# Encoder block in float32: half-size sums in DRAM for every second pair of w_down's rows, made during gate and up; fewer of h's sums through one buffer

## The chip, the cores and the metric

One core of one Trainium2 chip. The metric is the device time in microseconds of one execution; the kernel before has a median of 1118.89 us over three runs (1118.12 to 1121.63).

## What is computed

One block of a bidirectional encoder with 256 tokens and 16 meta tokens, width 2048, all in float32. Attention (neighbourhood attention in 8 heads, latent attention in 8 heads, an output projection) is followed by a gated MLP with 5632 inner columns, which is what the change touches:

```python
def conv_glu(x, w_gate, w_up, conv_w, conv_b, w_down):
    g = x @ w_gate
    u = x @ w_up
    ...
    for i in range(CONV_W):
        gc = gc + conv_w[i] * gp[:, i:i + L]
    return (jax.nn.silu(gc) * u) @ w_down

h = h + mix @ w_out[l]
h = h + conv_glu(rmsnorm(h, ffn_norm_g[l]), w_gate[l], w_up[l], conv_w[l], conv_b[l], w_down[l])
```

## The kernel before

**Splits.** TensorE multiplies in a float32 form of lower precision, so each operand is split into a high and a low part and each product becomes two or three matmuls. Every weight goes through one pipeline: SP issues a load of 512 KB into a buffer `raw` (128x1024), ACT copies it to `whi` (rounded), DVE subtracts to get `wlo`, TensorE uses both. There are five `raw` buffers, four `whi` and four `wlo`. When the MLP begins one more raw buffer is added (`more_raw`), and when gate and up no longer need the normed input, eight more (`halves`). A raw buffer is free again after DVE's subtraction.

**Strassen-like products.** Some parts of up (`w_up_s`, five groups of four column tiles, QUADS) and of down (`w_down_m`, 512 columns, called "mid"; `w_down_s`, 1024 columns, called "down") take seven products of sums in place of eight. The sums are of two kinds. Sums of values: `value_sums` takes four differences on DVE and splits them on ACT and DVE into a 128x1024 tile; for h (pairs 0 to 7 of its 16 tiles, `hl_sums`) and for the MLP's inner values (22 pairs, `pair_sums`). Most of these tiles are built in the one buffer `sums` (pool `combined`), stored to DRAM (`s_up`, `s_down`), and loaded again into `sin` (pool `s_parts`) when the products need them; `sums` is free when its store has landed. h's sums are also kept near, in the last columns of `act`, the tile of inner values, until those are written. That tile takes over the memory of attention's buffers, so it is there only from `ev_mlp` on. Before, pairs 0 to 5 (`EARLY = ST // 2`) go through `sums` and are loaded back into `act` after `ev_mlp`; pairs 6 and 7 wait for `ev_mlp` and are built in `act` itself.

Sums of weights (`weight_sums`): a row pair of `w_down_s` has four quarters of 512 columns. Two sums of neighbouring quarters are made in DRAM ahead of time (`sums_in_dram`): SP copies two quarters (512 KB) of the weights to a DRAM tile `early`, and a DMA issued on POOL adds the next two quarters to it (an accumulate). In the last stage the pair loads its lower quarters (512 KB, `lower`), one upper quarter (256 KB, `upper`) and the early tile (512 KB, `two`), and DVE makes two further sums of 128x512 in a fourth buffer (`more`).

**Stages.** Attention runs to about 395 us, with the output projection at its end; gate and up follow, with the groups of seven products spread among them; from about 765 us the 22 pairs of mid are spread among the last gate and up tiles; from about 955 us the 22 pairs of down stand among 13 of the 24 pieces of `w_down`'s other 512 columns (done the plain way), seven pieces having gone ahead, and the last four stand at the end. The copies and accumulates of `sums_in_dram` start in attention (first copy at 39 us, last accumulate at 378 us).

**What sets the order.** The kernel is written as threads that a small planner (`Flow`) runs with modelled costs: each instruction is recorded when the planner's clock of its engine says so, and all engines then run that order. So SP is one queue in a fixed order, and so are ACT and DVE: an instruction that waits holds all behind it. Threads with a low priority (3), such as h's sums, are recorded when nothing else is ready in the model, but in the chip they hold the engine like any other. A helper's line stands for all its uses: L243 is every ACT activation, L247 every DVE two-operand instruction, L283 and L661 to L663, L1955, L1956 the matmuls, L514 every load and store issued by SP, L716 the accumulate on POOL.

The waits on the small `scr` tiles in attention are copies between partitions that are issued on SP among the weight loads (rotary keys and queries); `sq8r` are squares of a head, which TensorE adds up.

## Time and profile before

| | |
|---|---|
| median of three runs | 1118.89 us (1118.12 to 1121.63) |
| the profiled execution | 1123.05 us, of which the span is 1121.2 |
| TensorE busy in the span | 98% |
| DVE, ACT, POOL busy | 90%, 67%, 13% |
| mean granted TensorE clock | 0.997 |
| DMA traffic | 275.57 MB, mean 246 GB/s |

A busy TensorE in this profile is not TensorE at its peak, since ends of matmuls are modelled; its waits are read from what ended them. "Idle before" stands in brackets behind an instruction, with what released it. A stage is read by the busy time of each engine in its window: where TensorE's has no gap, only work taken from TensorE or a faster clock can shorten the stage.

### The profile page before, as it was taken

What the parts mean: (1) busy time and instruction counts of PE and PEld (TensorE: products, weight loads), DVE (VectorE), ACT (ScalarE), POOL (GpSimd) and SP (SyncE); (2) the same over time, 40 slices, a digit from 0 to 9 for tenths busy, and PEclk for the clock granted to TensorE, in tenths of its full rate; (3) what the DMA queues carried; (4) which work ended last, traced back from release to release, by engine and by line L of the source; (5) the groups of instructions that cost most, each with busy time, mean ns of one, the idle gap of its engine ahead of it and who ended that gap; (6) DMA issues with size and microseconds to landing.
All of it is one profiled execution on the core that took longest, in us unless ns stands there. A gap on an engine that the chain in (4) does not pass through costs nothing.

```text
span 1121.2 us, 22349 instructions
## 1 busy us (share of the span) xinstructions
PE 1102.6 (98%) x8164; PEld 1048.7 (94%) x8164; DVE 1008.2 (90%) x1907; ACT 755.9 (67%) x1518; POOL 142.8 (13%) x216
## 2 busy tenths in 40 slices
PE   9989999999999989999999999999999999999998
PEld 9989999999999989999999999999999999787777
DVE  8869887988878879999999999999998989999896
ACT  8678978888647666656656556655665565666664
POOL 3221212232334400000000000000000000301012
PEclk9999999999999999999999999999999999999999
DMA  8666878687887888665756667567797889799991
GB/s 323 226 202 196 217 196 239 190 223 225 280 256 214 234 276 301 204 212 174 257 172 202 229 210 267 200 215 271 268 316 268 283 280 372 280 321 322 336 308 66
DMA packets 83318, 275.57 MB, mean 246 GB/s; under 512 B 9352, under 2 KB 13448, under 8 KB 83208
## 3 DMA queue, kind: packets, MB, share of 16 engines
q1 hardware_dynamic: 79752, 262.34, 68.3%
q0 software_dynamic: 3168, 11.54, 6.4%
q8 instruction: 64, 1.05, 0.4%
q14 instruction: 46, 0.38, 0.1%
q10 hardware_dynamic: 288, 0.27, 0.1%
HBM read 255.61 MB, written 40.89 MB: 264 GB/s over the span
## 4 chain that ended last, share of the span: by engine, by line
PE 73%; DVE 11%; DMA 9%; ACT 3%; issue 2%; SPq 1%; POOL 0%; DVEq 0%; ACTq 0%; POOLq 0%
PE bank L283 17%; PE bank L661 14%; PE bank L662 14%; PE bank L663 14%; PE bank L1955 8%; DVE wlo L247 7%; PE bank L1956 4%; PE bank L289 2%; DMA raw<-in_w_down_m 1%; DMA halves<-early 1%; DMA raw<-early 1%; ACT whi L243 1%; DMA scr<-scr 1%; DMA more_raw<-early 1%; DVE raw L247 1%
## 5 line engine op out<-in xcount | busy, mean ns | idle before, releaser
L243 ACT ACTIVATE whi<-raw 128x512 fp32r<-128x512 f32 (+2 forms) x511 | 381.1, 765 | 138.8 <-PE bank L662 49.2
L247 DVE TENSOR_TENSOR wlo<-raw,whi 128x512 fp32r<-128x512 f32 (+2 forms) x511 | 444.7, 891 | 26.5 <-ACT whi L243 25.4
L661 PE MATMUL bank<-hl,whi 128*128 128x258 f32 (+1 forms) x1208 | 347.8, 288 | 0.0
L662 PE MATMUL bank<-hl,whi 128*128 128x258 f32 (+1 forms) x1208 | 344.4, 285 | 0.0
L663 PE MATMUL bank<-hl,wlo 128*128 128x258 f32 (+1 forms) x1208 | 344.0, 285 | 0.2
L663 PEld LDWEIGHTS bank<-hl,wlo 128*128 128x128 f32 x1208 | 230.4, 191 | 0.9 <-DVE wlo L247 0.8
L662 PEld LDWEIGHTS bank<-hl,whi 128*128 128x128 f32 x1208 | 229.9, 190 | 0.1
L661 PEld LDWEIGHTS bank<-hl,whi 128*128 128x128 f32 x1208 | 229.0, 190 | 0.4
L283 PE MATMUL bank<-whi,act 128*128 128x256 f32 (+1 forms) x560 | 144.4, 308 | 0.0
L1955 PE MATMUL bank<-hl,whi 128*128 128x512 f32 x384 | 138.1, 398 | 0.0
L1956 PE MATMUL bank<-hl,wlo 128*128 128x256 f32 x384 | 108.4, 282 | 0.6 <-DVE wlo L247 0.6
L283 PEld LDWEIGHTS bank<-whi,act 128*128 128x128 f32 x560 | 98.9, 189 | 5.9
L271 POOL TENSOR_TENSOR mt<-mt,mt 128x256 f32<-128x256 f32 x3 | 3.5, 1168 | 675.6 <-ACT mt L243 675.6
L243 ACT ACTIVATE whi<-halves 128x1024 fp32r<-128x1024 f32 (+2 forms) x68 | 63.5, 944 | 37.7 <-PE bank L283 22.4
L1955 PEld LDWEIGHTS bank<-hl,whi 128*128 128x128 f32 x384 | 72.9, 190 | 15.1
L283 PE MATMUL bank<-wlo,act 128*128 128x256 f32 (+1 forms) x280 | 86.2, 308 | 0.0
L283 PE MATMUL bank<-whi,sin 128*128 128x256 f32 (+1 forms) x312 | 85.0, 326 | 0.1
L247 DVE TENSOR_TENSOR wlo<-halves,whi 128x1024 fp32r<-128x1024 f32 (+2 forms) x68 | 75.0, 1124 | 1.0 <-ACT whi L243 0.6
L1956 PEld LDWEIGHTS bank<-hl,wlo 128*128 128x128 f32 x384 | 73.2, 191 | 0.9 <-DVE wlo L247 0.9
L243 ACT ACTIVATE whi<-more_raw 128x1024 fp32r<-128x1024 f32 (+2 forms) x60 | 51.6, 868 | 23.1 <-PE bank L283 6.4
L247 DVE TENSOR_TENSOR wlo<-more_raw,whi 128x1024 fp32r<-128x1024 f32 (+2 forms) x60 | 58.5, 987 | 3.2 <-ACT whi L243 3.2
L283 PEld LDWEIGHTS bank<-whi,sin 128*128 128x128 f32 x312 | 55.3, 188 | 6.1 <-issue 0.3
(301 smaller groups left out, 2166.9 us busy)
## 6 DMA issues: line engine op xcount, KB each, us to landing
raw<-in_w_gate SPq DMA_DIRECT2D x72, 512.0 KB, 5.5
raw<-in_w_in SPq DMA_DIRECT2D x52, 512.0 KB, 4.8
raw<-in_w_up SPq DMA_DIRECT2D x39, 512.0 KB, 6.0
sin<-s_down SPq DMA_DIRECT2D x36, 512.0 KB, 6.3
raw<-in_w_out SPq DMA_DIRECT2D x32, 512.0 KB, 5.9
raw<-in_w_up_s SPq DMA_DIRECT2D x32, 512.0 KB, 4.5
early<-in_w_down_s SPq DMA_DIRECT2D x22, 512.0 KB, 6.4
early<-in_w_down_s POOLq DMA_DIRECT2D x22, 512.0 KB, 7.9
```

The costliest lines, as they stand in the source:

```text
L243: nc.scalar.activation(out, in_, f, **kw)
L247: nc.vector.tensor_tensor(out, a, b, op)
L271: nc.gpsimd.tensor_tensor(out, a, b, op)
L283: nc.tensor.matmul(o, l, r, start=start, stop=stop)
L289: nc.tensor.transpose(o, i, ident[:n, :n])
L661: nc.tensor.matmul(ps, whi, xhi, start=start, stop=False)
L662: nc.tensor.matmul(ps, whi, xlo, start=False, stop=False)
L663: nc.tensor.matmul(ps, wlo, xhi, start=False, stop=stop)
L1955: nc.tensor.matmul(ps, whi, x, start=start, stop=False)
L1956: nc.tensor.matmul(ps[:, :n], wlo, x[:, 0, :], start=False, stop=stop)
```

## The change

- The DRAM sums start at `ev_mlp`, not in attention, with 18 us between steps, not 12.
- Pairs of `w_down_s` with an odd number ("third") have one early sum of 512 columns (256 KB copied, 256 KB added). It is loaded into the first half of `upper`, the raw upper quarter into the second, as two loads of 256 KB; the load of `two` goes, and DVE makes three sums of 128x512, not two. Even pairs are as before ("both").
- `EARLY = 4`: h's pairs 4 and 5 no longer go through `sums` and DRAM into `act`; they take a raw buffer as before, wait for `ev_mlp` in a thread of their own and are built in `act`, as pairs 6 and 7 are. They are stored afterwards.
- The sums of the last two pairs of values are used from where they were built in the mid stage: pair 20 from `sums`, pair 21 from a `sin` buffer (before: pair 21 alone, from `sums`).
- The last six mid pieces and the seven plain pieces ahead of down are ordered "mmdmmdddmmddd" (m mid, d plain), not "mmdmdmdmdmddd".
- The planner takes 2600 ns, not 2000, for a load's landing after 400 us of its clock, and counts the accumulates' traffic. Quarters have other product orders in "third" pairs; `MID_SUMS = 0` leaves the same for mid unused.

```diff
-MID_LEAD, MID_LEFT, MID_GAP = 4, 6, 2
+THIRD = 2
+MID_SUMS = 0
+EARLY_PACE = 18000.0
+LANDING = 2600.0
+MID_LEAD, TAIL = 4, "mmdmmdddmmddd"
...
+            if r.mode == "both":
+                yield "sp", 600
+                load(r.at["upper"][:, :q], r.src[:, :q], r.first_loaded, nc.sync)
+            else:
+                src, done = early_sums[r.g]
+                yield done
+                yield "sp", 600
+                load(r.at["upper"][:, :q], src, Event(), nc.sync)
+                yield "sp", 600
+                load(r.at["upper"][:, q:], r.src[:, :q], r.first_loaded, nc.sync)
...
                 yield r.first_loaded
+                yield from TT(m[:, :q], up[:, :q], up[:, q:], ALU.add)
+                r.used("upper")
+                yield from TT(m[:, q:], m[:, :q], low[:, q:], ALU.add)
+                yield from TT(t[:, :q], m[:, :q], low[:, :q], ALU.subtract)
...
+    for g in range(FC // 2):
+        ev, q, w = Event(), PW // 2, io["w_down_s"][g]
+        if g % THIRD:
+            t = dpool.tile([P, q], F32, name=f"early{g}")
+            early.append((t, w[:, q : 2 * q], w[:, 2 * q : 3 * q], ev))
+        else:
+            t = dpool.tile([P, PW], F32, name=f"early{g}")
+            early.append((t, w[:, : 2 * q], w[:, q : 3 * q], ev))
...
-            fl.cur.t += 12000.0
+            fl.cur.t += EARLY_PACE
...
-        yield pieces[18].loaded
-        fl.spawn(sums_in_dram())
...
         fl.set(ev_mlp)
+        fl.spawn(sums_in_dram())
...
-    EARLY = ST // 2
+    EARLY = 4
...
+            if EARLY <= i < ST // 2:
+                fl.spawn(hl_pair(i, v, ab), 3)
+            else:
+                yield from hl_pair(i, v, ab)
+    def hl_pair(i, v, ab):
+        if i >= EARLY:
+            yield ev_mlp
+        yield from value_sums(*saved_sums["up"][i], *ab, near[i])
...
-            parts = yield from one(combined)
+            parts = yield from one(s_parts if last == [LAST] else combined)
```

What the planner makes of it, at three places. First SP in attention, where the third early copy stood ahead of four scr copies. Before:

```order
L514 DMA raw1_81<-in_w_kv_up 128x512
L514 DMA raw2_82<-in_w_in 128x1024
L514 DMA raw3_83<-in_w_in 128x1024
L514 DMA early2_137<-in_w_down_s 128x1024
L514 DMA scr8_184<-scr6_182 32x258 x4
L514 DMA raw4_84<-in_w_in 128x1024
```

The same place of the change:

```order
L540 DMA raw1_81<-in_w_kv_up 128x512
L540 DMA raw2_82<-in_w_in 128x1024
L540 DMA raw3_83<-in_w_in 128x1024
L540 DMA scr1_177<-scr7_183 32x258 x4
L540 DMA raw4_84<-in_w_in 128x1024
```

The copy is gone and the scr copies stand behind weight loads alone; as in all of attention, buffer numbers differ.

Second ACT where the MLP begins; `s_2` is the norm's scale, `resT` the residual, `raw` with `res` the gained h of a pair. Before:

```order
L243 ACTIVATE parts_sq0_194<-kr_202 128x258
L243 ACTIVATE raw4_84<-res4_4086,vecs_94 128x256
L243 ACTIVATE whi3_88<-raw2_82 128x1024
L243 ACTIVATE resT4_5374<-bank7_79 128x512
L243 ACTIVATE sums0_93<-raw4_84 128x256
L243 ACTIVATE s_2_165<-scr8_184 128x258
L243 ACTIVATE s_2_165<-s_2_165 128x258
L243 ACTIVATE scr3_179<-s_2_165 128x258
L243 ACTIVATE sums0_93<-raw4_84 128x256
L243 ACTIVATE whi0_85<-raw3_83 128x1024
```

The same place of the change:

```order
L247 ACTIVATE parts_sq0_194<-kr_202 128x258
L247 ACTIVATE raw4_84<-res4_4043,vecs_94 128x256
L247 ACTIVATE whi3_88<-raw2_82 128x1024
L247 ACTIVATE resT4_5329<-bank7_79 128x512
L247 ACTIVATE s_2_165<-scr3_179 128x258
L247 ACTIVATE s_2_165<-s_2_165 128x258
L247 ACTIVATE scr4_180<-s_2_165 128x258
L247 ACTIVATE raw2_82<-res5_4056,vecs_94 128x256 x2
L247 ACTIVATE whi0_85<-raw3_83 128x1024
```

Pair 4's two splits into `sums` no longer stand around the scale; those of pairs 1 to 3 stand ahead of these rows in both. Pair 5's gain moves one weight split earlier and holds its buffer, with pair 4's, until `act` is there.

Third DVE in the last stage, an even and an odd pair of the change:

```order
L251 TENSOR_TENSOR raw4_84<-raw4_84,halves3_11164 128x512
L251 TENSOR_TENSOR raw2_82<-halves2_11125 128x512
L251 TENSOR_TENSOR raw2_82<-raw2_82,halves2_11125 128x512
L251 TENSOR_TENSOR halves1_11086<-raw2_82,halves2_11125 128x512
L251 TENSOR_TENSOR wlo0_89<-halves3_11164,whi0_85 128x1024
L251 TENSOR_TENSOR wlo1_90<-halves1_11086,whi1_86 128x512
```

The first row is the second sum of an even pair; the next three are an odd pair's, where before there were two.

192 lines of the change are left out of this document (121 added, 71 removed).

## The prediction

> **What bounds the kernel now.** I read the page's first two sections, then the busy time by stage, then what TensorE waits for. Columns of the stage rows: window in us, length, then busy time and instruction count of PE, PEld (its weight loads), DVE, ACT and POOL, granted TensorE clock, DMA share, GB/s.
>
> ```profile
> span 1121.2 us, 22349 instructions
> PE 1102.6 (98%) x8164; PEld 1048.7 (94%) x8164; DVE 1008.2 (90%) x1907; ACT 755.9 (67%) x1518; POOL 142.8 (13%) x216
> ```
> ```profile
> 40.00:100.00 60.00, 56.94 (x450) 56.00 (x449) 46.81 (x125) 45.99 (x133) 10.02 (x20) 0.97 0.65 199
> 395.00:420.00 25.00, 22.04 (x139) 19.86 (x139) 18.63 (x36) 18.21 (x34) 0.30 (x1) 0.93 0.83 269
> 420.00:520.00 100.00, 100.00 (x779) 97.23 (x778) 93.90 (x175) 63.64 (x101) 0.00 (x0) 1.00 0.67 228
> 520.00:620.00 100.00, 100.00 (x809) 98.58 (x809) 98.33 (x180) 63.65 (x100) 0.00 (x0) 1.00 0.63 208
> 620.00:720.00 100.00, 99.61 (x770) 96.17 (x770) 96.14 (x182) 61.02 (x102) 0.00 (x0) 1.00 0.65 226
> 720.00:780.00 60.00, 59.91 (x469) 58.10 (x468) 58.31 (x106) 37.08 (x59) 0.00 (x0) 1.00 0.70 242
> 780.00:833.00 53.00, 53.00 (x387) 50.38 (x387) 51.12 (x95) 32.81 (x53) 0.00 (x0) 1.00 0.83 283
> ```
> ```profile
> 955.00:1095.00 140.00, 136.46 (x630) 109.53 (x629) 129.25 (x143) 91.09 (x105) 16.89 (x13) 1.00 0.90 318
> ```
> ```profile
> PE bank L283 <- DVE sq8r L259: 3.8, 3, 2.8
> PE bank L283 <- DVE wlo L247: 3.3, 5, 1.3
> ```
>
> TensorE bounds it nearly everywhere: in gate and up (420 to 780) it never rests, and DVE, at 94 to 98 of 100 us, keeps up only just. So no edit can win more than TensorE's waits and its slow clock. The waits sit in three places: one in attention (sq8r, 2.8), one where the MLP begins (3 us, rows in part 2), five small ones in the last stage (wlo, 3.3 together). The two rows above give TensorE's waits for one instruction each: sum, times, longest. The granted clock is below 1 in two rows: 0.03 x 60 = 1.8 us and 0.07 x 25 = 1.75 us, right behind the two long waits. The profiled execution took 1123.05 us, the span and 1.85 around it, 4.2 over the median of 1118.89.
>
> **1. Attention: DRAM sums leave it.** The long wait:
>
> ```profile
> 76.43 0.17 PE L283 MATMUL bank<-ones_r,sq8r 128*4 128x2 f32 x1 [2.82 <-DVE sq8r L259]
> 76.83 0.22 PE L283 MATMUL bank<-ones_r,sq8r 128*4 128x2 f32 x3 [0.24 <-POOL sq8r L271]
> ```
> ```profile
> 67.65 6.96 DMA scr<-scr
> ```
> ```profile
> 64.78 0.52 SPq L514 DMA_DIRECT2D early<-in_w_down_s  x1
> 65.82 2.42 SPq L514 DMA_DIRECT2D scr<-scr  x4
> ```
>
> TensorE rests 2.82 + 0.24 = 3.06 us because four small scr copies land late. A 512 KB early copy stood just ahead of them on SP, and an accumulate was issued on POOL beside them. The first row below gives the landing of these four, the second that of the next group, which had no early copy directly ahead.
>
> ```profile
> DMA to landing us min/median/max: 5.5/6.9/7.4
> ```
> ```profile
> DMA to landing us min/median/max: 3.7/4.8/5.2
> ```
>
> Medians differ by 2.1 us, and the early copy's issue (0.52) is gone as well: about 2.6 us sooner, bounds 0.5 (most of the wait is the weight loads ahead) and 3.06 (all). I take 2.3. Elsewhere in attention the order shifts by a few rows; TensorE's other waits there are about 1 us of sq8r. I take 0.5 gained, bounds -3 (one new wait like the old) and +2.
>
> **2. Where the MLP begins.** ACT rows first, with the wait in brackets, then DVE, then TensorE, then the chain.
>
> ```profile
> 369.31 0.42 ACT L243 ACTIVATE sums<-raw 128x256 fp32r<-128x256 f32 x1 [4.03 <-DMA s_up<-sums]
> 394.64 0.72 ACT L243 ACTIVATE sums<-raw 128x256 fp32r<-128x256 f32 x2 [1.81 <-DMA s_up<-sums]
> 403.22 0.42 ACT L243 ACTIVATE sums<-raw 128x256 fp32r<-128x256 f32 x1 [2.02 <-DMA s_up<-sums]
> ```
> ```profile
> 369.76 0.42 DVE L247 TENSOR_TENSOR sums<-raw,sums 128x256 fp32r<-128x256 f32 x1 [2.16 <-ACT sums L243]
> ```
> ```profile
> 399.42 0.39 PE L283 MATMUL bank<-parts_sq,ones_r 128*128 128x258 f32 x1 [2.06 <-ACT parts_sq L243]
> 400.71 0.39 PE L283 MATMUL bank<-parts_sq,ones_r 128*128 128x258 f32 x1 [0.90 <-DVE parts_sq L247]
> ```
> ```profile
> 387.36 7.19 DMA s_up<-sums
> ```
> ```profile
> DMA to landing us min/median/max: 6.8/7.3/9.1
> ```
>
> The last row gives the landing of the four saves from 360 to 396. Every pair of h's sums waits until the one `sums` buffer is saved, 7 us, and the weight splits behind it on ACT and DVE wait too. The edit frees pairs 4 and 5, so the 2.02 at 403 goes; but the waits that reach TensorE at 397 are those of pairs 1 to 3 (4.03 to 1.81), which keep the buffer. What helps these is the traffic that leaves: an accumulate, issued at 361.61, ran beside the first save, the one of 9.1 us, and POOL's issues slow DVE, which runs without a pause from 369.76 on:
>
> ```profile
> 355.94 0.75 DVE L247 TENSOR_TENSOR res<-res,scr 128x258 f32<-128x258 f32 x2
> 361.04 1.25 DVE L247 TENSOR_TENSOR res<-res,scr 128x258 f32<-128x258 f32 x2
> 372.05 0.88 DVE L255 SCALAR_TENSOR_TENSOR hl<-res,vecs,hl 128x258 fp32r<-128x258 f32 x2
> 376.93 1.38 DVE L255 SCALAR_TENSOR_TENSOR hl<-res,vecs,hl 128x258 fp32r<-128x258 f32 x2
> 302.53 3.86 DVE L247 TENSOR_TENSOR wlo<-raw,whi 128x512 fp32r<-128x512 f32 x3
> ```
> ```profile
> 361.61 0.79 POOL L716 DMA_DIRECT2D early<-in_w_down_s  x1
> 377.57 0.80 POOL L716 DMA_DIRECT2D early<-in_w_down_s  x1
> ```
>
> At each issue the same DVE pair takes 0.50 us more (1.25 against 0.75, 1.38 against 0.88). DVE comes 0.5 us earlier by the second issue and up to 2.16 by a faster first save; of TensorE's 2.06 + 0.90 = 2.96 us I take 2.2 as gained, bounds 0 and 2.96. Against it: pairs 4 to 7 now hold up to four weight buffers together while four 512 KB reloads and the first early copy queue, where before it was six reloads. Up to four split pieces of 24 products at 100/809 = 0.124 us, 11.9 us of TensorE's work, cover this; without them a late load would cost 2 us.
>
> **3. The slow clock.** It followed each rest of about 3 us and cost 3.55 us here; the rest of 1.3 us, in a row with clock 1.00, had none behind it. If 1 and 2 hold, both go. The profiled execution is 4.2 over the median, so I suppose that the median execution has it once: 1.8 gained, bounds 0 and 3.55. [...]
>
> **4. Gate and up take the DRAM sums.** In DMA time:
>
> ```profile
> q1 hardware_dynamic: 79752, 262.34, 68.3%
> q0 software_dynamic: 3168, 11.54, 6.4%
> ```
>
> An accumulate takes 6.4% x 1121.2 / 22 = 3.26 us of all 16 engines; a copy at q1's rate (262.34 MB in 766 us) 1.53, at most 3.26. With half the bytes in every second pair that is 22 x 0.75 x 4.8 = 79 us over 24 steps of 18 us: +0.18 on shares of 0.63 to 0.70. It fits, except from 780 to 833, where 0.83 + 0.18 is over 1. On DVE 22 issues cost 22 x 0.50 = 11 us. One a step is 5.6 per 100 us, 2.8 us, against idle time of 6.1, 1.7, 3.9 and (per 100) 2.8 and 3.5 in the rows above: DVE falls 1.1 us behind between 520 and 620 and recovers in the next row, inside the 11.9 us that it can work ahead. SP pays 0.52 a copy, which waits for nothing; the weight loads behind it start that much later, which the same pieces cover. POOL has no other work there. I take 1.0 lost in all, bounds 0 and 6 (79 us of DMA at the one tenth that doesn't fit from 780 on gives 5 of it). [...]
>
> **5. The last stage.** In every second pair a read of 256 KB goes (11 x 0.26 MB = 2.9 MB, 8.4 us at q1's rate) and one sum of 128x512 comes:
>
> ```profile
> L247 DVE TENSOR_TENSOR halves<-halves,raw 128x512 f32<-128x512 f32 x9 | 6.2, 686 | 2.1 <-DMA raw<-early 2.0
> ```
> ```profile
> DVE halves L247 <- DMA halves<-early: 4.5, 4, 1.5
> DVE halves L247 <- DMA raw<-early: 3.3, 2, 2.0
> DVE halves L247 <- DMA more_raw<-early: 1.1, 1, 1.1
> ```
>
> DVE gains 11 x 0.69 = 7.5 us of work and has 140 - 129.25 = 10.75 idle, 8.9 of it the waits above for early sums. Where these waits go, the work fits and TensorE's 3.3 us of waits go too; where they stay, it ends 7.5 - 1.85 = 5.6 later. DMA at 0.90 falls to 0.84, so I take 1.0 gained, bounds -5.6 and +3.3. The last values' sums in place and the order of the 13 pieces ahead of the stage cost nothing: TensorE shows no wait between 860 and 955, and ready pieces hide them; uncovered, one load of 7 us.
>
> **Sum.** 2.3 + 0.5 + 2.2 + 1.8 - 1.0 + 1.0 = 6.8 under the median: 1112. Against the profiled execution, with the whole 3.55, it is 8.55: 1114.5.
>
> **The rivals.**
> - *The waits stay.* The copies and saves are late because of weight loads ahead of them, not of early traffic, and pairs 1 to 3 keep the one buffer, so that the edit frees none that matters. For it: 7.19 at 387, when no accumulate ran. Then 1, 2 and 3 give nothing: 1118.9 - 0.5 = 1118.4.
> - *DVE becomes the bound in gate and up (slower).* Next to an issue at 303 three splits took 3.86 us, where three of 128x512 take 3 x 0.69 = 2.1 (the mean in part 5): 1.8 us lost, with POOL additions beside it. At 1.5 us an issue, 8.3 per 100 us, DVE would fall behind by 2.2 + 6.7 + 4.5 + 3.3 + 2.5 = 19 us in the five rows; half of the 11.9 of lead covers 6, 13 reach TensorE: 1118.9 - 7.8 + 13 = 1124. It reaches TensorE from about 1 us an issue (lateness 8.2, over the 6) and makes the kernel slower from about 1.25. Against it: POOL has no additions there.
> - *Everything goes*: 3.06 + 2.96 + 3.55 + 2 + 3.3 = 14.9: 1104.
>
> **Chances and range.** Forecast (1107 to 1115.5) 0.53, better 0.14, waits stay 0.20, slower 0.13. About 0.3%, 3.4 us, is what a measurement can tell from no change: faster 0.67, same 0.20, slower 0.13. The range runs from the best case, 1103.5, to 1122.5, short of the slower rival.
>
> **What would show it.** Right: scr copies landing in about 5 us and no clock below 1 at 77 and 402; ACT's waits for s_up under 2 us; DVE pairs longer by 0.5 at POOL's issues, with TensorE's count per 100 us unchanged; no DVE wait on early sums. Wrong: a gap of TensorE in gate and up, a new rest of 3 us in attention, or DVE without idle time behind 955.

## The result and the profile after

| | before | change |
|---|---|---|
| median of 20 runs each | 1121.62 us (1118.12 to 1124.88) | 1120.34 us (1118.23 to 1121.86) |
| profiled execution | 1123.05 us, span 1121.2 | 1118.23 us, span 1116.4 |
| ratio to before | | 0.9984, 95% interval 0.9974 to 0.9994 |

The change is faster by 0.16% (0.06 to 0.26% by the interval), less than the 0.3% that the prediction counted as no change. Six to seven us were forecast. The profiles are 4.8 us of span apart, the medians 1.3: the profiled execution of before lies 1.4 over its median, that of the change 2.1 under. Stages are read from one profiled execution of each kernel, so differences of a us or two between them are not safe; ratios decide.

**By stage.** The span is cut at three starts that each trace has: the first up product, the first down product 512 wide, the last such product.

| us | to the first up product | gate, up, change to down | last stage | behind it |
|---|---|---|---|---|
| before | 396.8 | 562.8 | 144.2 | 17.4 |
| change | 389.9 | 560.4 | 149.2 | 16.9 |
| difference | -6.9 | -2.4 | **+5.0** | -0.5 |

Attention and the MLP's begin gained, and the last stage gave most of it back. Two views of the change follow (L287, L251, L275 and L540 are before's L283, L247, L271 and L514; `bank` is where TensorE writes its results, `SPq` is SP's queue): TensorE's waits (sum, times, longest), and the stages (window, length, busy time and count of PE, PEld, DVE, ACT, POOL, granted clock, DMA share, GB/s).

```profile
PE bank L287 <- DVE wlo L251: 6.5, 4, 5.4
PE bank L712 <- DVE wlo L251: 1.6, 3, 0.7
PE bank L287 <- DMA sin<-s_up: 1.5, 1, 1.5
PE bank L837 <- DVE em L834: 1.1, 1, 1.1
PE bank L287 <- DVE parts_sq L251: 0.8, 1, 0.8
PE bank L293 <- DVE more_raw L251: 0.6, 1, 0.6
PE bank L287 <- POOL sq8r L275: 0.5, 2, 0.3
```
```profile
40.00:100.00 60.00, 59.47 (x477) 57.90 (x476) 49.19 (x134) 48.35 (x140) 8.04 (x18) 1.00 0.49 160
395.00:420.00 25.00, 25.00 (x177) 23.39 (x177) 24.02 (x56) 19.32 (x38) 0.98 (x1) 1.00 0.97 344
520.00:620.00 100.00, 99.60 (x788) 97.22 (x787) 95.63 (x171) 63.11 (x99) 4.08 (x5) 1.00 0.82 261
620.00:720.00 100.00, 97.25 (x764) 94.44 (x763) 96.80 (x187) 60.20 (x99) 4.10 (x5) 1.00 0.81 255
955.00:1095.00 140.00, 132.84 (x607) 107.47 (x606) 128.19 (x142) 86.72 (x100) 21.98 (x9) 0.98 0.81 284
1000.00:1030.00 30.00, 24.56 (x105) 19.77 (x105) 23.48 (x28) 16.17 (x19) 12.35 (x3) 0.90 0.73 251
```

The sq8r wait of 2.8 us is down to 0.3 and the clock at 40 to 100 back at 1.00; at 395 to 420 TensorE has no gap left. New are small waits in gate and up (L712, sin, more_raw) and one long wait, 5.4 of the first row's 6.5 us. It lies at 1020, where TensorE is busy for 24.56 of 30 us and the clock falls to 0.90. Its cause is in the chain of the change around it (start, us, what):

```profile
1006.87 10.97 POOL mt L275
...
1019.40 0.34 SPq L2015
...
1019.85 3.82 DMA halves<-early
...
1023.69 0.70 DVE halves L251
```

POOL's addition for the stored output takes 10.96 us. In the profile of before the same instruction took 0.99 us. The two rows, first the change, then before:

```profile
1006.87 10.96 POOL L275 TENSOR_TENSOR mt<-mt,mt 128x256 f32<-128x256 f32 x1 [47.29 <-ACT mt L247]
```
```profile
1016.93 0.99 POOL L271 TENSOR_TENSOR mt<-mt,mt 128x256 f32<-128x256 f32 x1 [46.88 <-ACT mt L243]
```

SP issues the store of that output (L2015) and all loads, in one order. While the store waits for POOL (this addition and two short instructions behind it), no load is issued for 11 us:

```profile
1008.39 0.38 SPq L540 DMA_DIRECT2D sums<-s_down  x1
1019.40 0.34 SPq L2015 DMA_DIRECT2D outT<-mt  x1
1019.85 0.37 SPq L540 DMA_DIRECT2D halves<-early  x1
```

The early sum that this load brings lands at 1023.67, and DVE, which had run without a pause until 1017.24, waits for it:

```profile
1016.02 1.22 DVE L251 TENSOR_TENSOR wlo<-raw,whi 128x1024 fp32r<-128x1024 f32 x1
1023.69 0.69 DVE L251 TENSOR_TENSOR halves<-raw,halves 128x512 f32<-128x512 f32 x1 [6.46 <-DMA halves<-early]
```

POOL's addition ends 0.59 us behind DVE's last instruction (1006.87 + 10.96 - 1017.24): it looks shut out for as long as DVE runs on. That is the theory to test; its rival is that DVE is simply full, by the 11 additional sums.

### The profile page after: what moved, and what is told of

It reads as the page before. It is cut to its first block, busy times and chain, and to the rows that moved or that the text cites. A ratio compares the mean times of both kernels' runs of the same rounds, so it can differ in the third digit from the quotient of the medians.

```text
span 1116.4 us, 22345 instructions
## 1 busy us (share of the span) xinstructions
PE 1099.7 (99%) x8164; PEld 1048.3 (94%) x8164; DVE 1012.1 (91%) x1918; ACT 754.1 (68%) x1518; POOL 157.6 (14%) x216
## 4 chain that ended last, share of the span: by engine, by line
PE 64%; DVE 19%; DMA 7%; ACT 6%; issue 3%; POOL 1%; SPq 0%; DVEq 0%; ACTq 0%; POOLq 0%
PE bank L287 17%; PE bank L712 11%; PE bank L710 11%; PE bank L711 11%; DVE wlo L251 10%; PE bank L2026 7%; PE bank L2027 4%; DVE raw L251 3%; ACT whi L247 3%; DVE mt L251 2%; PE bank L293 2%; DMA s_up<-sums 1%; POOL mt L275 1%; DMA halves<-early 1%; ACT scr L247 1%
## 5 line engine op out<-in xcount | busy, mean ns | idle before, releaser
L247 ACT ACTIVATE whi<-raw 128x512 fp32r<-128x512 f32 (+2 forms) x510 | 383.8, 770 | 164.5 <-PE bank L711 58.0
L251 DVE TENSOR_TENSOR wlo<-raw,whi 128x512 fp32r<-128x512 f32 (+2 forms) x510 | 444.8, 891 | 32.2 <-ACT whi L247 29.5
L712 PE MATMUL bank<-hl,wlo 128*128 128x258 f32 (+1 forms) x1208 | 343.2, 284 | 1.2 <-DVE wlo L251 1.1
L712 PEld LDWEIGHTS bank<-hl,wlo 128*128 128x128 f32 x1208 | 229.7, 190 | 1.9 <-DVE wlo L251 1.8
L287 PE MATMUL bank<-whi,act 128*128 128x256 f32 (+1 forms) x560 | 146.7, 309 | 0.0
L287 PEld LDWEIGHTS bank<-whi,act 128*128 128x128 f32 x560 | 99.5, 190 | 6.2
L287 PE MATMUL bank<-wlo,act 128*128 128x256 f32 (+1 forms) x280 | 86.6, 309 | 0.0
L287 PE MATMUL bank<-whi,sin 128*128 128x256 f32 (+1 forms) x304 | 85.1, 327 | 1.5 <-DMA sin<-s_up 1.5
L247 ACT ACTIVATE whi<-halves 128x1024 fp32r<-128x1024 f32 (+2 forms) x68 | 61.9, 930 | 34.6 <-PE bank L287 19.3
L779 POOL DMA_DIRECT2D early<-in_w_down_s x22 | 18.1, 825 | 426.2 <-DMA early<-in_w_down_s 410.2
L251 DVE TENSOR_TENSOR wlo<-halves,whi 128x1024 fp32r<-128x1024 f32 (+2 forms) x68 | 72.2, 1088 | 2.7 <-ACT whi L247 2.6
L247 ACT ACTIVATE whi<-more_raw 128x1024 fp32r<-128x1024 f32 (+2 forms) x61 | 50.8, 844 | 30.8 <-PE bank L287 13.9
L287 PEld LDWEIGHTS bank<-whi,sin 128*128 128x128 f32 x304 | 53.9, 188 | 7.6 <-ACT mt L247 1.6
L251 DVE TENSOR_TENSOR wlo<-more_raw,whi 128x1024 fp32r<-128x1024 f32 (+2 forms) x61 | 57.7, 957 | 1.2 <-ACT whi L247 1.1
```

What stands on the lines that cost most here:

```text
L247: nc.scalar.activation(out, in_, f, **kw)
L251: nc.vector.tensor_tensor(out, a, b, op)
L287: nc.tensor.matmul(o, l, r, start=start, stop=stop)
L712: nc.tensor.matmul(ps, wlo, xhi, start=False, stop=stop)
L779: nc.gpsimd.dma_start(t, src, accum_op=ALU.add)
```

## The experiments

Ratios are to the kernel before on the same chip.

**1 and 2. The store on POOL's queue**, in the change and in the kernel before, so that SP's loads no longer stand behind it.

```diff
-        yield "sp", 600
-        nc.sync.dma_start(io["outT"][:, m, :], o_)
+        yield "pool", 1000
+        nc.gpsimd.dma_start(io["outT"][:, m, :], o_)
```

> The change, with the stores of the plain columns (outT) issued on POOL behind the additions that they wait for, not on SP. Theory 'starved addition': in the last stage DVE runs two-input instructions without a gap, the addition on POOL waits for one (10.97 us at 1007), and the store that waits for it holds SP and all weight loads behind it (none issued from 1008.4 to 1019.4). Then the addition stays long here, but the loads go on: TensorE's wait of 5.4 us and the half clock behind it go, 5 to 7 us less than the change. Rival 'DVE is full': the 7.5 us of sums added to DVE in the last stage are what TensorE waits for, so the wait only moves: within 1.5 us of the change.

> The kernel before with the same stores issued on POOL. Both theories: its additions took 1.0 to 1.5 us there and held nothing, so within 1.5 us of the kernel before. If the gain of the other run came from something general in the store's queue, this one would be faster by several us too.

Measured: the change with it 0.9936 (0.9915 to 0.9957), 1115.03 us; before with it 1.0005 (0.9992 to 1.0018). POOL's first addition stayed shut out, 11.57 us, but nothing stood behind it:

```profile
1008.09 11.57 POOL L275 TENSOR_TENSOR mt<-mt,mt 128x256 f32<-128x256 f32 x1 [47.30 <-ACT mt L247]
```

The last stage went from 149.2 to 143.9 us. The held queue cost the change 5.3 us and the kernel before nothing that can be told.

**3. Full-size sums** in every pair (`-THIRD = 2`, `+THIRD = 1`).

> The change with full-size DRAM sums for all 22 pairs (THIRD = 1): 11 sums of 128x512 less on DVE in the last stage (7.5 us), 2.9 MB more read there, a quarter more DRAM sums in gate and up. Starved addition: DVE waits for early sums again (8 us or so), POOL finds gaps and its additions take 1 to 3 us; no wait of 5 us, and 1 to 4 us less than the change. DVE is full: the same direction, but the waits spread over the stage shrink as well, 4 to 6 us less.

Measured: 0.9915 (0.9894 to 0.9936), 1112.88 us. Last stage 139.9 us, POOL's addition 1.37 us, gate and up 565.5 (5.1 more than the change). It is 7.5 us under the change, more than either theory had named, and so decides nothing between them. What it shows is that the size of the sums made the last stage long; experiment 7 adds that their place did not.

**4. Six of h's sums ahead of the MLP** (`-EARLY = 4`, `+EARLY = ST // 2`).

> The change with six of h's pairs through the one buffer again (EARLY = 6). The prediction's reading: the waits that reached TensorE where the MLP begins were those of pairs 1 to 3 and went with the DRAM sums' traffic, so TensorE's wait there stays at about 1 us and the time within 1 us of the change. Rival: the freed buffer made the gain; then about 3 us of wait, a clock of a half and 3 to 5 us more than the change.

Measured: 1.0014 (1.0000 to 1.0029), 1123.85 us, 3.5 more than the change. My expectation missed: the first up product was as early (390.0), but gate and up took 564.4 us, 4.0 more; of TensorE's waits 1.6 us lay at 395 and the rest later. (The last stage of this profile is 2.4 us longer as well, 151.6; of the 6.9 us between the two profiles the medians show 3.5.)

**5. The last stage's plain additions on DVE** (`-PTT`, `+TT` at three places), the store left on SP.

> The change with the plain columns' additions (three per column tile of 128x256, two tiles in the last stage and one ahead of it) on DVE, not POOL; the store stays on SP. Starved addition: about 3 us more work on DVE, but SP is never held for long, so the wait of 5 us goes: 2 to 6 us less than the change. If the store's place on SP were harmful by itself, or DVE simply full, the wait would stay or grow: 0 to 3 us more than the change.

Measured: 0.9893 (0.9873 to 0.9912), 1110.56 us. DVE gets work, and the kernel becomes 10 us faster, where I had expected 2 to 6. The stage's row and TensorE's first wait of this kernel:

```profile
955.00:1095.00 140.00, 137.86 (x653) 113.00 (x652) 134.62 (x156) 92.44 (x106) 4.19 (x3) 1.00 0.82 285
```
```profile
PE bank L287 <- DVE wlo L251: 2.4, 3, 1.4
```

DVE is busy for 134.62 of 140 us against 128.19 in the change, and TensorE for 5 us more. The last stage takes 141.2 us. "DVE is full" has fallen.

**6. The kernel before with nothing but its sums moved** to the MLP's begin, one each 18 us.

```diff
-            fl.cur.t += 12000.0
+            fl.cur.t += 18000.0
...
-        yield pieces[18].loaded
-        fl.spawn(sums_in_dram())
...
+        fl.spawn(sums_in_dram())
```

> The kernel before with one part of the change alone: the DRAM sums, full size, start where the MLP begins, 18 us a step. The prediction's parts 1 to 3: TensorE's wait of 3 us at 73 us goes to under 1, that at the start of the MLP to 1 to 2, the clock is never halved in these places; 5 to 8 us less than before, less what gate and up lose to the moved traffic (1 by the prediction, about 3 as the change's trace looks). Rival 'traffic is innocent': the waits stay, within 1 us of before.

Measured: 1.0137 (1.0111 to 1.0163), 1139.55 us. A clear miss. The first up product came at 390.3, as forecast, but gate, up and the change to down took 587.4 us, 24.6 more, in many small waits. The row of one stage of it:

```profile
520.00:620.00 100.00, 95.85 (x752) 93.42 (x751) 92.36 (x170) 59.49 (x94) 3.27 (x4) 0.98 0.79 246
```

DMA has a share of 0.79 only, so there is room; yet TensorE rests for 4 of 100 us. The same full-size sums at the same pace cost the kernel of experiment 3 far less (565.5 us there), so something else in the change pays for them.

**7. The change with its sums back in attention** at their old pace of 12 us.

> The change with its DRAM sums (half-size in every second pair) back in attention, 12 us a step. If moving the sums made the gain up to the MLP, TensorE reaches its first up product at 395 to 397 us, not 390, and gate and up take less than the 560.4 us of the change because no DRAM traffic stands beside the loads; the last stage keeps its long addition. In all 0 to 4 us more than the change.

Measured: 0.9964 (0.9949 to 0.9979), 1118.71 us. The first up product at 394.2 (4.3 later than in the change), gate and up 556.3 (4.1 less). I had expected 0 to 4 us more than the change; it is 1.6 less, and the two intervals overlap. The move gains in one place what it loses in the other. POOL's addition again took 10.96 us, the last stage 149.6.

**8. POOL additions beside kinds of DVE instructions**, measured by themselves; the kernel leaves out the encoder block. A seventh section, behind those below, is `two_inputs` again.

```python
for work in (None, two_inputs, two_sizes, chained, one_input, from_psum):
    start()      # one short DVE product, from which ScalarE makes POOL's input
    adds()       # three POOL instructions, 128x256
    if work:
        work()   # 14 to 24 DVE instructions of this kind
...
```

> Not the block: seven sections in which three additions of 128x256 on POOL, one after the other, start while DVE runs one kind of instruction for about 15 us (its output is not the reference's). Starved addition: alone each takes about 0.75 us; beside back-to-back independent DVE instructions with two inputs in SBUF the first takes over 5 us; beside DVE instructions with one input, or one input in PSUM, 1 to 2 us; beside chained ones, which leave a small gap, 1 to 2. DMA issues on POOL lengthen no DVE instruction. Rival 'a general slowness of POOL': the first takes as long in all sections.

Measured: alone 0.72 us; beside one-input DVE work 1.19; beside DVE work with a PSUM input 0.72; beside chained two-input work 0.72. Beside independent two-input work the first addition took 1.12 us in one section and 15.63 and 15.88 in two others:

```profile
11.88 1.12 POOL L52 TENSOR_TENSOR o<-t,t 128x256 f32<-128x256 f32 x1 [1.05 <-ACT t L49]
29.70 15.63 POOL L52 TENSOR_TENSOR o<-t,t 128x256 f32<-128x256 f32 x1 [13.36 <-ACT t L49]
96.80 15.88 POOL L83 TENSOR_TENSOR o<-t,t 128x256 f32<-128x256 f32 x1 [12.35 <-ACT t L49]
```

Both long ones end 0.58 us behind DVE's stream, as in the change. The shut-out is real, and not certain: the first and the third row stand beside the same 14 instructions. That issues on POOL lengthen no DVE instruction was not measured here, since they came up only when DVE's stream had ended.

**9. The planner's two new numbers taken back** in the change.

```diff
-LANDING = 2600.0
+LANDING = 2000.0
...
-                dma_free[0] = max(dma_free[0], fl.cur.t) + 8 * P * size(t) / 350.0
```

> The change with its two new numbers in the planner taken back: a load is reckoned to land 2.0 us after its bytes are through, in gate and up too (LANDING 2000, not 2600), and the sums in DRAM are no longer reckoned into the DMA engines' time. The work is the same, only the order of the instructions on each engine changes. Theory A (the planner's reckoning matters once the sums run in gate and up: it then orders DVE's and TensorE's work for loads that really come later, and this is much of the 24 us that the kernel before lost in gate and up when its sums were moved there alone): gate, up and the change to down longer than the change's 560.4 us by 4 us or more, the time 1123 to 1135 us. Theory B (that loss came from the twice larger sums and from six, not four, of h's sums before the MLP): within 1.5 us of the change's 560.4 there, the time 1117 to 1122 us.

Measured: 1.0028 (1.0015 to 1.0042), 1125.68 us; gate, up and the change to down 569.7 us, 9.3 more than the change, the last stage 146.5. Theory A holds: two numbers that add no instruction are worth 5 us in all, 9 in gate and up. The sums are half-size here too, and POOL's first addition took 2.66 us only (POOL's row, then DVE's around its pause):

```profile
1017.45 2.66 POOL L275 TENSOR_TENSOR mt<-mt,mt 128x256 f32<-128x256 f32 x1 [48.02 <-ACT mt L247]
1018.28 1.22 DVE L251 TENSOR_TENSOR wlo<-halves,whi 128x1024 fp32r<-128x1024 f32 x1
1021.04 1.15 DVE L251 TENSOR_TENSOR halves<-halves 128x512 f32<-128x512 f32 x1 [1.53 <-DMA halves<-in_w_down_s]
```

It ends 0.61 us behind DVE's last instruction, as in the change; DVE paused at 1019.50 for a late load. So the 11 us need both edits: the half-size sums, and an order of DVE's instructions without a pause. The last stage is 2.3 us longer than before's even so.

**10. Full-size sums, and back in attention**: of the change only h's sums, the tail and the planner's numbers are left (`THIRD = 1`, `EARLY_PACE = 12000.0`, the start as in experiment 7).

> The change with full-size sums in every pair (THIRD 1) and the sums back in attention at their old pace: what is left of the change is four of h's sums through one buffer, the tail's order and the planner's numbers. If the parts add up as the stages of the runs so far say, the first up product is at 394.2 us (sums in attention, as in the run that moved only these back), gate and up take 556.3 us (as there), the last stage 139.9 us (as with full-size sums in gate and up) and 18 us lie behind it: a span of about 1108, a time of 1107 to 1113 us. Rival: the last stage was short in the other run with full-size sums only because its late start (955.4 us) had given the sums' loads more time; then it takes about 144 us, as before, and the time is 1112 to 1117 us.

Measured: 0.9884 (0.9864 to 0.9904), 1110.02 us, with 393.8, 556.7 and 139.9 us in the stages. All three were forecast to half a us from runs with one edit each: the size and the place of the sums add up.

**11. Full-size sums from 195 us on**, one each 14 us (`THIRD = 1`, `yield pieces[62].loaded`, `EARLY_PACE = 14000.0`).

> As the run with full-size sums in attention, but begun at about 195 us, behind the copies between buffers at 65 to 75 and 180 us that TensorE waited for, at one sum each 14 us, so that about half of them lie in attention from 195 us and half in gate and up. If attention's loss is that of the wait at 73 us alone, the first up product is near 391 us; if the sums near 397 us also cost, near 393 us. If gate and up lose by the number of sums in them, they take 558 to 561 us here (between 556.3 without and 565.5 with all of the full-size sums). With 140 us for the last stage: 1105 to 1111 us. Rival (full-size sums cost gate and up their 5 us through a few of them, at one place): 565 us there, the time 1111 to 1116 us.

Measured: 0.9914 (0.9890 to 0.9937), 1112.82 us; stages 389.7, 563.7, 139.8. Attention is as hoped; gate and up lose 7.0 us against experiment 10, by waits at 423 to 477 and one of 1.0 at 548. Ten of the 22 accumulates lie behind 390 us, and they cost 7.0 us against 8.8 for all of them in experiment 3: not by their number, as the rival had it (565, 1111 to 1116), and mostly where the MLP begins.

**12. The tail's order and the last values' sums taken back** in the change (`TAIL = "mmdmdmdmdmddd"`, only the last pair kept in place, its rank).

> The change with the last three pieces taken back: the order of the loads at the end of the middle's down products (m and d by turns again), the place of the sums of the last pair but one (saved and read again, not used in the buffer where they were made), and these sums' rank. The prediction counted this at nothing. Theory: within 1.5 us of the change, 1117 to 1122 us, with POOL's first addition of the last stage still 8 us or longer. Rival (the order at the end is what makes DVE gapless at 1003 to 1017 us, by bringing the last stage's work forward): POOL's addition 1 to 2 us, the last stage 140 to 145 us, the time 1111 to 1116 us; or, the pieces being there for a wait of their own, the change to down longer by 2 us or more and the time over 1123 us.

Measured: 0.9995 (0.9981 to 1.0009), 1122.01 us, POOL's addition 11.07 us, last stage 150.3. The intervals of this and of the change overlap: nothing that the runs can tell.

**13. The kernel before with the landing time alone.**

```diff
-        fl.set(ev, t + 2000.0 - fl.cur.t)
+        fl.set(ev, t + (2000.0 if fl.cur.t < 4e5 else 2600.0) - fl.cur.t)
```

> The kernel before with one number changed: from the MLP on the planner reckons that a load lands 2.6 us after its bytes are through, not 2.0. No instruction is added or removed; the order of DVE's, ScalarE's, TensorE's and SP's instructions behind 400 us changes. The first up product stays at 396.8 us in either case. Theory (the landing time is the edit that gains): gate, up and the change to down shorter than before's 562.8 us by 3 to 6 us, as in the run with full-size sums in attention (556.7), the last stage by 2 to 4 us (139.9 there), the time 1112 to 1117 us. Rival (it matters only in the company of the others, since its reckoning stands in for the sums' traffic in gate and up, which the kernel before does not have): within 1.5 us of the kernel before.

Measured: 0.9941 (0.9924 to 0.9957), 1114.51 us. One number, with as many instructions on every engine, gains what the whole change was forecast to gain. Stages 398.0, 559.6, 139.9. What it does, first in the kernel before, then with the number (DVE rows, the wait in brackets):

```profile
973.39 1.21 DVE L247 TENSOR_TENSOR wlo<-halves,whi 128x1024 fp32r<-128x1024 f32 x1
975.57 0.69 DVE L247 TENSOR_TENSOR raw<-raw,halves 128x512 f32<-128x512 f32 x1 [0.97 <-DMA halves<-early]
976.18 1.22 DVE L247 TENSOR_TENSOR wlo<-raw,whi 128x1024 fp32r<-128x1024 f32 x1
```
```profile
971.36 1.22 DVE L247 TENSOR_TENSOR wlo<-halves,whi 128x1024 fp32r<-128x1024 f32 x1
972.49 1.21 DVE L247 TENSOR_TENSOR wlo<-raw,whi 128x1024 fp32r<-128x1024 f32 x1
973.63 0.68 DVE L247 TENSOR_TENSOR raw<-raw,halves 128x512 f32<-128x512 f32 x1
```

Before, the sum that waits for its load stands ahead of a split that is ready; a planner that expects the load later puts the split first, and the wait is gone. TensorE's wait for these splits goes from 3.3 us to 0.4, and the last stage is 4.3 us shorter with full-size sums:

```profile
PE bank L283 <- DVE wlo L247: 0.4, 1, 0.4
```

**14 to 16. Three edits in experiment 10's kernel**: the landing time back at 2.0 us; six of h's sums; the plain additions on DVE.

> The run with full-size sums in attention (1110.0 us), with the landing time back at 2.0 us. If the landing time carries the gain in gate and up: they go from 556.7 back to 560 to 564 us, the last stage from 139.9 to 142 to 145 us, the time 1115 to 1120 us. Rival (the smaller set of h's sums and the order of the tail carry it): within 1.5 us of 1110.0.

> The run with full-size sums in attention (1110.0 us), with six of h's sums ahead of the MLP, not four (EARLY 6, the buffer and the rest as before). If the freed pairs matter at the MLP's begin, where the prediction counted them at nothing: the first up product back from 393.8 to 395.5 to 397 us, TensorE's wait there again 2 to 3 us; in the change itself the same edit cost 4.0 us in gate and up and nothing at the begin. Theory: 2 to 4 us longer in all, 1112 to 1114 us. Rival (the prediction: the waits there are those of the pairs 1 to 3): within 1 us of 1110.0.

> The run with full-size sums in attention (1110.0 us), with the plain additions of the last stage on DVE, not on POOL. In that run POOL's first addition took 1.80 us, not 10.96, so there is no shut-out to take away, and DVE gets six more additions, about 3 us of work in all. Theory (the shut-out alone made the loss): no gain, 1109 to 1112 us. Rival (POOL's additions cost DVE or the store's wait on SP something anyway, 1 to 3 us): 1107 to 1109 us, the fastest kernel of all.

Measured: the landing time back 0.9960 (0.9943 to 0.9976), 1116.68 us, stages 393.0, 560.1, 144.1. So the landing time carries 4.2 of the 4.3 us that the last stage had gained against before, and 3.4 of the 6.1 in gate and up. Six of h's sums 0.9904 (0.9886 to 0.9921), 1110.55 us: nothing that can be told, against my theory; the first up product stayed at 393.8. Additions on DVE 0.9882 (0.9865 to 0.9898), 1108.40 us, last stage 139.2: the lowest median, and within the rival's range, yet the ratio and its interval are those of experiment 10. Where POOL isn't shut out, moving its additions gains nothing that can be told.

**17. All full-size sums between 195 and 395 us**, one each 9 us (experiment 11 with `EARLY_PACE = 9000.0`).

> The run with full-size sums begun at about 195 us, at one sum each 9 us, not 14, so that nearly all of the 22 lie between 195 and 400 us: behind the copies that TensorE waited for up to 196 us, and ahead of gate and up. Theory (the place of the sums costs, and this stretch has time to spare): the first up product at 389.7 to 391 us, gate and up 556 to 558 us, the last stage 140 us, a time of 1104 to 1108 us, the fastest kernel. Rival (the sums cost by their traffic wherever they lie, and denser ones more): the first up product at 393 us or later, the time 1109 to 1114 us.

Measured: 0.9962 (0.9944 to 0.9981), 1117.30 us; stages 391.4, 566.7, 138.8. Both expectations missed: the time is above the rival's 1109 to 1114 too. The pace was not kept: the last sums ran until about 440 us, across the MLP's begin, and there the DMA engines were full (a share of 1.03 from 390 to 440). The landing of what SP issued at 386 to 400 us, weight loads and saves for the most part, first here, then in experiment 10, whose sums were done by then:

```profile
DMA to landing us min/median/max: 10.2/12.3/14.4
```
```profile
DMA to landing us min/median/max: 3.3/4.7/6.1
```

So the rival's mechanism, late loads by traffic, is what the trace shows, at a place where traffic was dense already (before has a share of 0.84 from 390 to 420 and 0.89 from 420 to 440). That the free stretch of attention would carry the sums at no cost stays untested.

**18. What lets POOL in**, by the number of DVE instructions since DVE's last pause; this kernel too leaves out the encoder block.

```python
e <- o * s              # DVE, waits for POOL's addition of the section before
lead x (y <- x - x)     # DVE, two inputs, 128x256 or 128x1024
d <- s * s              # DVE; ScalarE copies it for POOL
14 x (y <- x - x)       # DVE, two inputs, 128x1024
o <- t + t              # POOL, 128x256
```

> Not the block: ten sections that leave it out. In each, DVE first waits for POOL's addition of the section before, then runs two-input instructions without a pause: a number of short ones (128x256: 2, 5, 6, 7, 8, 9, 12; then 128x1024: 4, 6, 9), one that ScalarE waits for, and fourteen of 128x1024. ScalarE's result releases one POOL addition with two inputs of 128x256, which comes up in about the third DVE instruction behind the number, so when DVE has begun about 5, 8, 9, 10, 11, 12, 15 and 7, 9, 12 instructions since its pause, 2.5 to 6 us behind the pause in the first seven sections and 6 to 12 in the last three. Theory (the number of DVE's instructions since its last pause decides): at most 2.7 us in the sections of 5, 8, 9, 7 and 9, and 10 to 17 us, until DVE's stream ends, in the others. Rival (the time since the pause decides, at about 7.5 us): at most 2.7 us in all of the first seven, 10 us and more in the last two. Rival (neither: a matter of chance or of phase within DVE's instruction): no order by either.

Measured: the number and the time both fell. The first section (4 instructions behind the pause) let POOL in at 0.98 us; all other nine shut it out for 15.89 us, those of 7 instructions and of 3.36 us since the pause too. The first three sections:

```profile
11.39 0.98 POOL L59 TENSOR_TENSOR o<-t,t 128x256 f32<-128x256 f32 x1 [8.37 <-ACT t L56]
28.88 15.89 POOL L59 TENSOR_TENSOR o<-t,t 128x256 f32<-128x256 f32 x1 [16.51 <-ACT t L56]
48.16 15.89 POOL L59 TENSOR_TENSOR o<-t,t 128x256 f32<-128x256 f32 x1 [3.39 <-ACT t L56]
```

With experiment 8, in a stream of ready, independent two-input instructions POOL was shut out in 11 of 13 sections. The first section differs in one thing more: ScalarE loaded a table for 1.28 us there, so that POOL came up later, and the second has no pause of DVE ahead of it. The third expectation isn't excluded: POOL's addition came up 0.82 us into a DVE instruction in the first section and 0.67 us in the nine others, but in experiment 8 one that came up at 0.67 us got in. Where POOL got in, it waited for the running DVE instruction only and was done 0.66 us into the next, which took 1.75 us in place of 1.22. What decides between the two stays open.

## Why the prediction was wrong

The four medians with the other edits of the change in place show what its two main edits are worth:

| us | sums in attention | sums in gate and up |
|---|---|---|
| full size | 1110.02 (exp. 10) | 1112.88 (exp. 3) |
| half size in every second pair | 1118.71 (exp. 7) | 1120.34 (the change) |

Half size costs 7.5 to 8.7 us. The move costs 1.6 to 2.9, but the intervals of the two ratios overlap in each row. What the change gained came from the edits around them, about 12 us (experiment 10 against before), of which the landing time carries about 7 (experiments 13 and 14); h's sums and the tail carry nothing that can be told (15 and 12), and the rest is not assigned. So the small gain is two large terms that the sum did not have, one of each sign.

- **1, attention: right in sign, short in size, partly for another reason.** With the clock, 2.3 + 0.5 + 1.8 = 4.6 us were forecast to the first up product; 6.9 came. The scr copies land in 1.9 us, not in about 5. Of the 6.9, 3.9 are the move (393.8 in experiment 10 against 389.9). The other 3.0 came with the sums still in attention: the wait at 73 was gone there too, and with the landing time or six of h's sums taken back as well (393.0, 393.8). The edit left for it is the planner's reckoning of the sums' traffic; that is by elimination, not tried alone. The two don't add: the move without it gave 6.5 (experiment 6).
- **2, the MLP's begin: right in size, and by luck.** TensorE's 2.96 us became 0.8, so 2.2 gained as forecast, though ACT's wait for the saves stayed at 3.11 us, over the 2 named. But the traffic that leaves did little of it: with the move alone the waits there are 2.3 us (experiment 6), and with the sums still in attention and the other edits in, 0.9 (experiment 10). That pairs 4 and 5 don't matter holds with the sums in attention (experiment 15) and not in the change, where they cost gate and up 4.0 us (experiment 4).
- **3, the clock: right in these two windows**; neither is below 1.00 any more. The wait at 1020 brought a slow clock of its own (0.90 from 1000 to 1030), and the mean granted clock is 0.997 before and after.
- **4, gate and up: the total about right by luck, its terms wrong.** From the first up product to down the change gains 2.4 us. At 390 to 420 us TensorE's products run 4.0 us closer together (the wait and the clock), so 1.6 is lost behind it, against 1.0 forecast. But DVE paid nothing at POOL's issues: the 57 DVE instructions beside the 22 issues are 0.04 us longer in all than their like elsewhere. An issue at 462.76 lies within the first row below; the second row has none:

```profile
461.96 1.67 DVE L259 SCALAR_TENSOR_TENSOR mt<-mt,vecs,mt 128x256 f32<-128x256 f32 x4
480.31 1.67 DVE L259 SCALAR_TENSOR_TENSOR mt<-mt,vecs,mt 128x256 f32<-128x256 f32 x4
```
  The 0.50 us that attention showed at issues were not the issues' own. POOL's additions stood beside the same DVE pairs:

```profile
357.75 3.91 POOL L271 TENSOR_TENSOR kr<-kr,scr 128x258 f32<-128x258 f32 x2 [4.30 <-ACT scr L243]
372.59 5.03 POOL L271 TENSOR_TENSOR kr<-kr,scr 128x258 f32<-128x258 f32 x2 [6.66 <-ACT scr L243]
```
  Of the 50 DVE instructions beside an issue in before's attention, the 24 with no POOL computation beside them are 0.15 us longer in all, the 26 with one 6.6. The rows also show that POOL could be held up before the change: these pairs took 3.91 and 5.03 us, where two took 1.82 at 351.64. (Part 5 finds the same price of a POOL addition, 0.55 us, on DVE.) So the rival of a DVE bound by issues (1124) had no basis either. The loss came by TensorE's waits at 657, 693 and 714 us for splits and loads that came late. And the planner's numbers, at which I counted nothing, save 9.3 us here (experiment 9). Taken back one at a time from the change, these numbers (9.3), the size (5.1, experiment 3), h's sums (4.0, experiment 4) and the tail (1.4, experiment 12) make 19.8 of the 27.0 us between the change and experiment 6; the other 7 stay open.
- **5, the last stage: this step failed.** "DMA at 0.90 falls to 0.84, so I take 1.0 gained, bounds -5.6 and +3.3": 5.0 were lost. The size was within the bound by luck, for the mechanism was another. I added DVE's work against its idle time and named what is late next on DVE only. The engine that pays is POOL, held up for as long as DVE ran on (10.96 us), and behind POOL's addition stood a store, and behind the store every load (none issued for 11 us). With the additions off POOL the same half-size sums make a last stage of 141.2 us (experiment 5), 8.0 less, and with the store alone off SP 143.9 (experiment 1). But the gain that I forecast isn't there without that queue either: with full-size sums and the same planner the stage takes 139.2 to 139.9 us (experiments 16 and 3), so half size still loses 1.3 to 2.0 by these single profiles, and gains nothing. Before's 144.2 hides this, because the landing time alone takes it to 139.9 (experiment 13), a term that I put at nothing: the +5.0 is, in this order, -4.3 from that number and +9.3 from half size. The order matters: with half size already there, the planner's numbers lengthen the stage (146.5 without them, experiment 9), since DVE loses the pause in which POOL got in (its addition took 2.66 us without these numbers, 10.96 with them). Nor did DVE's waits for early sums go, as the gain required: 9.3 us in the change (6.5 of it behind the store), 9.9 before. In before POOL waited for one DVE instruction only: its addition, 0.99 us long, came up at 1016.93, within the first of the two below, and was done 0.68 us into the second, which took 1.23 us where such a split of 128x512 takes 0.68:

```profile
1016.10 1.22 DVE L247 TENSOR_TENSOR wlo<-more_raw,whi 128x1024 fp32r<-128x1024 f32 x1
1017.24 1.23 DVE L247 TENSOR_TENSOR wlo<-halves,whi 128x512 fp32r<-128x512 f32 x1
```
  In the change POOL's addition, 10.96 us long, didn't get its turn at any of the eleven DVE instructions that began while it waited. There the wait was not for one instruction but lasted until DVE's next pause; why POOL lost each turn is not shown.
- **"The last values' sums and the order of the pieces cost nothing"**: holds (experiment 12).
- **The sum.** Against the profile of before 8.55 us were forecast and 4.8 came: 6 us too much in step 5, 2.3 too little in step 1, the rest small. The rival "the waits stay" (1118.4) came nearest in number, and its mechanism is wrong: the waits at 73 and 397 us went.

## What to carry to other kernels

Before you put more work on an engine that has idle time, look at what other engines do beside it: here a short POOL instruction with two SBUF inputs waited for the whole of DVE's stream (10.96 us; 0.72 alone in experiment 8), and what stood behind it in SP's queue waited as well (no load for 11 us), so in this kernel a store that hangs on POOL didn't belong in the queue of the loads. And read a planner's constants as part of a change: here 0.6 us in a reckoned landing time moved instructions that wait behind such as are ready, and gained about 7 us, while the two visible edits together lost 10. When several edits come in one change, build each edit alone and all but each. The size and the place of the sums added up to half a us here; others did not: the move alone cost 24.6 us in gate and up (experiment 6), and h's sums 4.0 there in the change and nothing that can be told in experiment 15.

## What the runs showed of the hardware

- A 128x256 POOL addition that takes 0.72 us alone (experiment 8) took 2.66 (experiment 9), 10.96 (the change), 11.57 (experiment 1), 15.63 and 15.88 (experiment 8) and 15.89 us (experiment 18) beside DVE's ready two-input instructions. In the change and in experiments 1, 8 and 9 it ended 0.58 to 0.61 us behind the last DVE instruction ahead of DVE's next pause, one of 0.04 us in experiment 1. It was not always so: in before and in experiments 2, 3, 6, 10 and 11 it took 0.96 to 1.80 us. In before and in experiments 3 and 18 (0.98 us in the first section) it waited for the running DVE instruction and was done 0.66 to 0.68 us into the next, which took 0.53 to 0.55 us more in before and in experiment 18. Beside DVE work with one input in PSUM it took 0.72, beside one-input work 1.19 (experiment 8).
- 22 accumulate issues on POOL in gate and up did not lengthen DVE's instructions (0.04 us in all, in the change); in before's attention the same issues had stood beside 0.50 us, with POOL's additions running.
- The granted clock was 0.50 in or behind some of TensorE's waits: from 78 to 80 and from 402 to 405 us in before (waits of 2.82, and of 2.06 and 0.90 close together), from 1024 to 1030 in the change (5.4 at 1021). It was 0.93 from 395 to 420 in experiment 13, where TensorE rests for 1.89 us in all, and 0.97 from 720 to 780 in experiment 3, whose longest wait is 2.0. It was 1.00 over all of experiment 11, where TensorE rests for 2.38 us between 460 and 480, and 0.999 over all of experiment 2, whose longest wait is 3.2 (0.997 in before). So the length of a wait alone does not decide, and the prediction's "It followed each rest of about 3 us" is shown for its one execution only.
